# Decode attention interleaved with a feed-forward pass: scores in two runs per half batch, values in one, four buffers of turned keys

## The chip, the cores and the metric

The kernel runs on one core of one Trainium2 chip. The metric is the device time of one execution, in microseconds. The kernel before took 1261.52 us (median of 3 runs, 1261.35 to 1262.61). One more execution was recorded by the profiler; all rows below come from it.

## The reference

One layer of a hybrid decoder is computed for 512 prompt tokens and for 8 sample sequences of 4 new tokens each, with shared weights: a SwiGLU feed-forward pass, a mixer (four heads of a gated recurrence, four heads of latent attention), and a second feed-forward pass. The part that matters here is the latent attention of the sample tokens over 4096 cached positions, which lie in pages of 128:

```
past_c = cache_kv_latent[l][page_table].reshape(Bs, past_len, KV_LORA)    # 8 x 4096 x 256
past_r = cache_k_rope[l][page_table].reshape(Bs, past_len, QK_ROPE)       # 8 x 4096 x 64
...
s = (einsum('bqhr,bsr->bhqs', ql, c_kv) + einsum('bqhd,bsd->bhqs', qr, k_rope)) * scale
s = where(k_pos <= q_pos, s, -inf)
p = softmax(s, axis=-1)
return einsum('bhqs,bsr->bqhr', p, c_kv)
```

Each sequence has 16 query rows (4 tokens by 4 heads). A score row needs the 256 latent and 64 rotary elements of a cached position; the values are the same 256 latent elements. Everything is fp32.

## The kernel before, in words

Large products are made of fp32r pairs: each weight tile is loaded by SyncE into `wraw` (five buffers), cast by ScalarE into `wh` (line 248), and the rest is taken by VectorE into `wl` (line 249); three matmuls per 128 rows of the contraction then add up in a PSUM bank `acc` (lines 257, 275, 286). Four pairs of `wh` and `wl` are in rotation in the stage described here.

The decode attention is computed in a stage of its own, from about 715 to 985 us of the profiled span. There it is interleaved with the second feed-forward pass over the first 256 tokens. Two generators run side by side: `decode()` yields after each of its steps, and a loop calls the feed-forward generator `gb` so that 100 of its pieces are spread evenly over the first 94 decode steps. One piece is mostly 12 `acc` matmuls of 256 columns while gate and up columns are computed, and 15 or 18 while down columns are.

The cache is worked through in 16 half batches (class `Half`), each of 2048 positions of one sequence, held as two blocks of 128 partitions by 8 positions. For a half batch:

- `gather` starts two indirect DMAs from GpSimd per block: the rotary rows into `rraw` (four buffers, line 1360) and the latent rows into `craw` (line 1361), which rotates through seven slots that are taken over from tiles that are dead by then (`ulb`, `uhb`, `ha`, `hb`, `mb`, `q`, `dx`; the trace shows the slots' names).
- `turn(st)` transposes keys on VectorE in 32 by 32 squares into a `kh` tile (line 1370), two instructions for each of five steps. `JS` says which two of the ten groups of 32 elements a step turns; step 0 is the rotary pair, which reads `rraw`. `kh` has three buffers.
- `score(st)` multiplies one `kh` tile with the queries: 16 matmuls (32 in the trace, since each fp32 matmul is shown as two) that use the array as eight tiles of 64 rows by 32 columns (line 1382). They add up over the five steps in two banks `s`. After the last step ScalarE and VectorE copy the banks (line 1388) and VectorE takes a row maximum `mxh`.
- `peak` (lines 1394 to 1406) spreads the maxima with one matmul `pm`, reduces it, takes the exponential on ScalarE, transposes on VectorE into `pt`, and copies it in 16 small pieces into `pbuf`, 12 of them on ScalarE and 4 on VectorE.
- `value(c)` multiplies block `c` by the probabilities: 8 matmuls (16 in the trace) on four tiles of 128 rows by 32 columns (line 1415). After every second half batch `gathered` collects the sums (line 1423).

Half batches overlap. In an iteration of five steps, the half batch two iterations back is scored, one step of scores per decode step; the one three back has its `peak` in step 0 and its `value` in steps 3 and 4, and each `value` is followed by the gather of one further block. In every step one `kh` is turned for a score that comes three steps later. Within one engine instructions run in the order of a scheduler that starts from this written order and moves single instructions by its own estimate of readiness.

Of the kernel before, what the change touches and what calls it, by code (L numbers as in the profile page):

```python
# [8 lines left out]
F32 = mybir.dt.float32  # L9
# [8 lines left out]
P = 128  # L18
# [17 lines left out]
RD = 64  # L36
# [5 lines left out]
ROWS = 8  # L42
# [20 lines left out]
NW, WX = 2, 2  # L63
NDEC = 100
JS = ((8, 9), (0, 1), (2, 3), (4, 5), (6, 7))
KHB = 3
LEVELS = (32, 16, 8, 4, 2, 1)
CH = 64

# [39 lines left out]
def hybrid_step_kernel(  # L109
# [5 lines left out]
    nc = tc.nc  # L115
# [12 lines left out]
    def mk(shape, dt, tag, bufs=1, pool=None):  # L128
        return (pool or cur[-1]).tile(shape, dt, name=tag, tag=tag, bufs=bufs)
# [130 lines left out]
    def gemm(wt, act_):  # L260
        wh, wl, kt = wt
        acc = ps("acc", "acc")
        n = act_[0].shape[-1]
        mm3(acc[:, :n], [((wh[:, k], wl[:, k]), (act_[0][:, k], act_[1][:, k])) for k in range(kt)])
        return acc[:, :n]
# [139 lines left out]
    idx = mk([P, NBLK], I32, "idx")  # L405
# [147 lines left out]
    with scope("ffn0") as pool:  # L553
# [91 lines left out]
        l, r = [u[:, lo4] for u in ux], [u[:, hi4] for u in ux]  # L645
# [13 lines left out]
        for j in range(NF // 2):  # L659
# [14 lines left out]
            if j:  # L674
                H = [mk([P, 2, 2, W2], F32R, n, 3) for n in ("hh", "hl")]
# [16 lines left out]
        H = [mk([P, 2, 2, W2], F32R, n, 3) for n in ("hh", "hl")]  # L692
# [4 lines left out]
        if True:  # L697
            if True:
                sst.close()
                st = stg.enter_context(tc.tile_pool(name="st", bufs=1, side="right", reuse_waits="tile"))  # L700
# [72 lines left out]
    with scope("mix") as mx_:  # L773
# [293 lines left out]
        with scope("at2"):  # L1067
# [6 lines left out]
            with scope("kv"):  # L1074
# [46 lines left out]
                for g in range(2):  # L1121
                    w = weight([w_qr[2 * g + i] for i in range(2)], KQ)
                    a = [gemm(w, Q[x]) for x in BOTH]
# [171 lines left out]
    with scope("dec"):  # L1295
# [47 lines left out]
        NH2 = 2 * NB  # L1343

        class Half:
# [7 lines left out]
            def gather(self):  # L1353
                blk = 2 * self.n + len(self.craw)
                slot = slots[blk % len(slots)]
                craw = qt if slot == "q0" else mk([P, ROWS * R], F32, slot, pool=None if slot == "dx" else act)
                craw = craw[:, : ROWS * R].rearrange("p (a r) -> p a r", a=ROWS)
                rraw = mk([P, ROWS, RD], F32, "rraw", 4)
                off = bass.IndirectOffsetOnAxis(ap=idx[:, blk : blk + 1], axis=0)
                nc.gpsimd.indirect_dma_start(rraw.rearrange("p a r -> p (a r)"), None, pool_r, off)  # L1360
                nc.gpsimd.indirect_dma_start(craw.rearrange("p a r -> p (a r)"), None, pool_c, off)
                self.craw.append(craw)
                self.rraw.append(rraw)

            def turn(self, st):
                kh = mk([P, 2, ROWS, 2, 32], F32, "kh", KHB)
                j = JS[st][0]
                for g in range(2):
                    src = self.craw[g][:, :, j * 32 : j * 32 + 64] if j < 8 else self.rraw[g]
                    nc.vector.transpose(kh[:, g].rearrange("p a j k -> p a (j k)"), src)  # L1370
                self.kh.append(kh)
# [54 lines left out]
        def decode():  # L1426
            H = [Half(n) for n in range(NH2)]
            blocks = [h_ for h_ in H for _ in range(2)]
            ups = [(h_, st) for h_ in H for st in range(len(JS))]

            def gather(n=1):
                for h_ in blocks[:n]:
                    h_.gather()
                del blocks[:n]

            def turn():
                if ups:
                    h_, st = ups.pop(0)
                    h_.turn(st)

            for n in range(NH2 + 4):

                def at(k):
                    return H[n - k] if 0 <= n - k < NH2 else None

                for st in range(len(JS)):
                    if at(2):
                        at(2).score(st)
                    if n < 3 and st == 0:
                        gather(2 + n // 2)  # L1450
                    if st == 0 and at(3):
                        at(3).peak()
                    if st == 1 and at(4) and at(4).i:
                        at(4).gathered()
                    if st >= 3 and at(3):
                        at(3).value(at(4), st - 3)
                        gather()
                    if at(2) or n == 1 and st >= 2:
                        turn()
                    yield  # L1460

        def decode_end():
# [33 lines left out]
            nc.vector.tensor_copy(oT[1][:, NH:, HS[1] - TS :], o[:, :P].rearrange("p (h t) -> p h t", h=NH))  # L1496

        ga, gn = decode(), decode_new()
        na, ib = len(JS) * (NH2 + 2) + 4, 0
        for ia in range(na):  # L1500
# [189 lines left out]
```

## Time and profile before

| | |
|---|---|
| median of the runs | 1261.52 us |
| profiled execution, its own time | 1272.78 us |
| its span, first to last instruction | 1271.0 us |
| mean granted TensorE clock | 0.997 |
| TensorE matmul busy | 1246.2 us (98%) |
| VectorE busy | 983.3 us (77%) |
| ScalarE busy | 740.0 us (58%) |
| first and last score matmul | 719.7 and 970.6 us |

Busy time counts an engine's matmuls or operations as a union, not what they could do at their peak. TensorE's weight loads (PEld) overlap its matmuls (PE). A row of the timeline gives the start, the duration, the engine, the line and operation, output and inputs, and a count; in brackets stands the idle time before it and what ended it. "issue" means that nothing the profile shows was waited for.

### The profile page before, as it was taken

What the parts mean: (1) busy time and instruction counts of PE and PEld (TensorE: products, weight loads), DVE (VectorE), ACT (ScalarE), POOL (GpSimd) and SP (SyncE); (2) the same over time, 40 slices, a digit from 0 to 9 for tenths busy, and PEclk for the clock granted to TensorE, in tenths of its full rate; (3) what the DMA queues carried; (4) which work ended last, traced back from release to release, by engine and by line L of the source; (5) the groups of instructions that cost most, each with busy time, mean ns of one, the idle gap of its engine ahead of it and who ended that gap; (6) DMA issues with size and microseconds to landing.
All of it is one profiled execution on the core that took longest, in us unless ns stands there. A gap on an engine that the chain in (4) does not pass through costs nothing.

```text
span 1271.0 us, 30058 instructions
## 1 busy us (share of the span) xinstructions
PE 1246.2 (98%) x12390; PEld 1156.1 (91%) x12390; DVE 983.3 (77%) x1974; ACT 740.0 (58%) x1559; POOL 73.4 (6%) x80
## 2 busy tenths in 40 slices
PE   8999999999999999999999999999999999999997
PEld 7999999999999988889888887777777999999997
DVE  7897778888678888777776997888987868566665
ACT  7675545454566645547567655664655777554454
POOL 0000000000000000000001312222310000000000
PEclk9999999999999999999999999999999999999999
DMA  6233323332154222234224968768675626545451
GB/s 233 84 117 100 100 84 100 101 100 92 53 217 157 84 86 69 71 90 128 84 68 147 376 225 305 264 231 314 238 236 190 227 102 197 184 138 189 142 160 59
DMA packets 72969, 195.06 MB, mean 153 GB/s; under 512 B 12320, under 2 KB 27712, under 8 KB 68096
## 3 DMA queue, kind: packets, MB, share of 16 engines
q1 hardware_dynamic: 64368, 149.94, 36.4%
q0 software_dynamic: 7168, 41.95, 9.1%
q8 instruction: 97, 1.59, 0.5%
q10 hardware_dynamic: 1296, 1.26, 0.3%
q14 instruction: 40, 0.33, 0.1%
HBM read 183.45 MB, written 9.67 MB: 152 GB/s over the span
## 4 chain that ended last, share of the span: by engine, by line
PE 89%; ACT 5%; DVE 4%; issue 1%; DMA 0%; DVEq 0%; SPq 0%; ACTq 0%
PE acc L257 29%; PE acc L275 19%; PE dn L257 8%; PE Y L559 6%; PE X L559 4%; PE Z L559 4%; PE s L1382 4%; PE acc L715 3%; PE o L1415 3%; PE s L1195 1%; ACT wh L248 1%; PE acc L286 1%; PE pa L936 1%; DVE wl L249 1%; PE zx L824 1%
## 5 line engine op out<-in xcount | busy, mean ns | idle before, releaser
L248 ACT CAST wh<-wraw 128x1024 fp32r<-128x1024 f32 (+2 forms) x194 | 185.1, 956 | 179.2 <-PE acc L257 113.2
L249 DVE TENSOR_TENSOR wl<-wraw,wh 128x1024 fp32r<-128x1024 f32 (+2 forms) x194 | 214.7, 1108 | 88.1 <-ACT wh L248 85.6
L275 PE MATMUL acc<-uha,wh 128*128 128x256 f32 (+1 forms) x528 | 157.8, 300 | 0.9 <-ACT uha L205 0.9
L275 PE MATMUL acc<-ula,wh 128*128 128x256 f32 (+1 forms) x528 | 150.8, 286 | 0.0
L275 PE MATMUL acc<-uha,wl 128*128 128x256 f32 (+1 forms) x528 | 150.0, 285 | 0.1
L257 PE MATMUL acc<-uhb,wh 128*128 128x288 f32 (+1 forms) x432 | 128.0, 296 | 0.0
L257 PE MATMUL acc<-uhb,wl 128*128 128x288 f32 (+1 forms) x432 | 126.9, 295 | 1.0 <-DVE wl L249 0.7
L257 PE MATMUL acc<-ulb,wh 128*128 128x288 f32 (+1 forms) x432 | 127.5, 295 | 0.0
L275 PEld LDWEIGHTS acc<-uha,wh 128*128 128x128 f32 x528 | 99.4, 189 | 14.8 <-issue 13.2
L275 PEld LDWEIGHTS acc<-ula,wh 128*128 128x128 f32 x528 | 99.6, 189 | 1.4 <-issue 1.2
L275 PEld LDWEIGHTS acc<-uha,wl 128*128 128x128 f32 x528 | 99.4, 188 | 1.3 <-issue 0.7
L257 PEld LDWEIGHTS acc<-uhb,wl 128*128 128x128 f32 x432 | 81.2, 188 | 1.6 <-DVE wl L249 1.5
L257 PEld LDWEIGHTS acc<-uhb,wh 128*128 128x128 f32 x432 | 81.0, 187 | 0.2 <-ACT uhb L168 0.2
L257 PEld LDWEIGHTS acc<-ulb,wh 128*128 128x128 f32 x432 | 81.1, 188 | 0.1
L257 PE MATMUL dn<-hh,dh 128*128 128x272 f32 x256 | 74.3, 290 | 0.0
L257 PE MATMUL dn<-hh,dl 128*128 128x272 f32 x256 | 73.7, 288 | 0.0
L257 PE MATMUL dn<-hl,dh 128*128 128x272 f32 x256 | 73.6, 288 | 0.0
L1382 PE MATMUL s<-kh,q 64*32 64x128 f32 x2560 | 55.7, 275 | 0.9 <-issue 0.9
L1406 ACT COPY pbuf<-pt 32x64 f32<-32x64 f32 x192 | 46.5, 242 | 13.2 <-DVE pt L1402 10.5
L275 PE MATMUL acc<-uhb,wh 128*128 128x272 f32 x176 | 52.5, 298 | 0.0
L257 PE MATMUL acc<-hlb,wh 128*128 128x288 f32 x176 | 52.1, 298 | 0.0
L257 PE MATMUL acc<-hhb,wh 128*128 128x288 f32 x176 | 51.8, 298 | 0.0
(637 smaller groups left out, 3901.6 us busy)
## 6 DMA issues: line engine op xcount, KB each, us to landing
wraw<-w_u SPq DMA_DIRECT2D x66, 512.0 KB
wraw<-w_g SPq DMA_DIRECT2D x65, 512.0 KB
wraw<-w_d SPq DMA_DIRECT2D x40, 384.0 KB
wraw<-w_in SPq DMA_DIRECT2D x24, 512.0 KB
wraw<-w_d SPq DMA_DIRECT2D x32, 320.0 KB
wraw<-w_d SPq DMA_DIRECT2D x16, 512.0 KB
wraw<-w_o SPq DMA_DIRECT2D x16, 512.0 KB
g_S<-state SPq DMA_DIRECT2D x4, 512.0 KB
```

What stands on the lines that cost most here:

```text
L248: nc.scalar.copy(wh[:, :kt], w[:, :kt])
L249: nc.vector.tensor_tensor(wl[:, :kt], w[:, :kt], f32(wh[:, :kt]), op=ALU.subtract)
L257: nc.tensor.matmul(out, a, b, start=n == 0, stop=n == last)
L275: nc.tensor.matmul(acc[:, :n], a[:, k], b[:, k], start=k + i == 0, stop=k == kt - 1 and i == 2)
L286: nc.tensor.matmul(acc, a[:, k], b[:, k], start=k + i == 0, stop=k == kt - 1 and i == 2)
L559: nc.tensor.matmul(bank, a[p][:, k], b[q][:, k], start=first and k + n == 0, stop=k == 3 and n == 2, skip_group_check=True)
L715: nc.tensor.matmul(accs[x, d], wts[d][p][:, k], hs[k // 2][q][:, k % 2, x], start=k + n == 0, stop=k == nf - 1 and n == 2)
L824: nc.tensor.matmul(z, w[a][:, k], U[1][b][:, k], start=k + n == 0, stop=k == KD - 1 and n == 2)
L936: nc.tensor.matmul(po[es, c].rearrange("p (n m) -> p n m", m=m), kx[:, cs], up(qx[:, cs], m), start=True, stop=True, skip_group_check=True)
L1382: nc.tensor.matmul(self.s[r][c * 32 : c * 32 + 32, :P], q[rs, j], kh, start=st + jj == 0, stop=st == len(JS) - 1 and jj == 1, skip_group_c ...
L1406: (nc.scalar.copy if g else nc.vector.tensor_copy)(self.p[g * 32 : g * 32 + 32, c // 2, c % 2 * 4 : c % 2 * 4 + 4, self.i * 16 : self.i * ...
L1415: nc.tensor.matmul(o[g : g + 32, :R], self.p[:, c, a], self.craw[c][:, a], start=i + c == 0 and a < 4, stop=i + c == 2 and a >= 4, skip_gr ...
```

## The change

The scores of a half batch are no longer computed one step at a time. Steps 0, 1 and 2 are computed together in decode step 2, and steps 3 and 4 together in decode step 4, so that `kh` has to hold more tiles: four buffers instead of three. `peak` moves from decode step 0 to step 1. Both `value` calls move to decode step 4, one right after the other, each still followed by the gather of one block. The rotary rows are gathered in a function of their own, both blocks at once, after the rotary pair of the half batch before has been turned; `rraw` has two buffers instead of four. Turning starts one step earlier in iteration 1, and pauses for two steps in iteration 2.

```diff
-KHB = 3
+KHB = 4
+PEAK = 1
+RUNS = {2: (0, 1, 2), 4: (3, 4)}
...
-                rraw = mk([P, ROWS, RD], F32, "rraw", 4)
                 off = bass.IndirectOffsetOnAxis(ap=idx[:, blk : blk + 1], axis=0)
-                nc.gpsimd.indirect_dma_start(rraw.rearrange("p a r -> p (a r)"), None, pool_r, off)
                 nc.gpsimd.indirect_dma_start(craw.rearrange("p a r -> p (a r)"), None, pool_c, off)
                 self.craw.append(craw)
-                self.rraw.append(rraw)
+
+            def gather_r(self):
+                for blk in (2 * self.n, 2 * self.n + 1):
+                    rraw = mk([P, ROWS, RD], F32, "rraw", 2)
+                    off = bass.IndirectOffsetOnAxis(ap=idx[:, blk : blk + 1], axis=0)
+                    nc.gpsimd.indirect_dma_start(rraw.rearrange("p a r -> p (a r)"), None, pool_r, off)
+                    self.rraw.append(rraw)
...
                     h_.turn(st)
+                    if st == 0 and h_.n + 1 < NH2:
+                        H[h_.n + 1].gather_r()
...
                 for st in range(len(JS)):
                     if at(2):
-                        at(2).score(st)
+                        for k in RUNS.get(st, ()):
+                            at(2).score(k)
                     if n < 3 and st == 0:
+                        if n == 0:
+                            H[0].gather_r()
                         gather(2 + n // 2)
-                    if st == 0 and at(3):
+                    if st == PEAK and at(3):
                         at(3).peak()
                     if st == 1 and at(4) and at(4).i:
                         at(4).gathered()
-                    if st >= 3 and at(3):
-                        at(3).value(at(4), st - 3)
-                        gather()
-                    if at(2) or n == 1 and st >= 2:
-                        turn()
+                    if st == len(JS) - 1 and at(3):
+                        for c in range(2):
+                            at(3).value(at(4), c)
+                            gather()
+                    if n > 1 or n == 1 and st >= 1:
+                        if n != 2 or st >= 2:
+                            turn()
                     yield
```

On TensorE, the stretch from the fifth peak matmul to the values of that half batch stood like this before (each `...` is a stretch of `acc` matmuls of the feed-forward pass, of 12 or 24):

```order
L1394 MATMUL pm<-ident,mxh 128x128
...
L1382 MATMUL s<-kh,q_8177 32x128 x16
L1423 MATMUL o<-q_8177,q_8811 128x32 x2
...
L1382 MATMUL s<-kh,q_8177 32x128 x16
...
L1382 MATMUL s<-kh,q_8177 32x128 x16
L1415 MATMUL o<-uhb,pbuf 32x256 x8
...
L1382 MATMUL s<-kh,q_8177 32x128 x16
L1415 MATMUL o<-ha,pbuf 32x256 x8
```

and stands like this now:

```order
L1400 MATMUL pm<-ident,mxh 128x128
L1429 MATMUL o<-q_8177,q_8811 128x32 x2
...
L1388 MATMUL s<-kh,q_8177 32x128 x48
...
L1388 MATMUL s<-kh,q_8177 32x128 x32
L1421 MATMUL o<-uhb,pbuf 32x256 x8
L1421 MATMUL o<-ha,pbuf 32x256 x8
```

The number of matmuls is the same; 16 score matmuls that stood apart are now runs of 48 and 32, and the two value runs touch. Over the whole program the 1280 score matmuls stand in 80 runs before and in 37 now; the first half batch is still cut into five, since the scheduler places its runs between other work.

On VectorE, the stretch of the seventh peak, from the reduction of `pm` to the copies into `pbuf`, stood like this before:

```order
L1396 TENSOR_REDUCE q_8177<-pm 128x16
L1370 STREAM_TRANSPOSE kh<-ulb 128x512
L1399 SCALAR_TENSOR_TENSOR mq,mbd<-q_8177 128x16
L1370 STREAM_TRANSPOSE kh<-uhb 128x512
L1370 STREAM_TRANSPOSE kh<-ulb 128x512
L1402 STREAM_TRANSPOSE pt<-q_8177 128x256
L1424 COPY q_8811<-o 128x4x16
L1406 COPY pbuf<-pt 32x4x16 x4
L1370 STREAM_TRANSPOSE kh<-uhb 128x512
```

and now:

```order
L1402 TENSOR_REDUCE q_8177<-pm 128x16
L1430 COPY q_8811<-o 128x4x16
L1405 SCALAR_TENSOR_TENSOR mq,mbd<-q_8177 128x16
L350 TENSOR_TENSOR sil<-acc,rna 128x256
L1408 STREAM_TRANSPOSE pt<-q_8177 128x256
L1412 COPY pbuf<-pt 32x4x16 x4
L1376 STREAM_TRANSPOSE kh<-ulb 128x512
L1376 STREAM_TRANSPOSE kh<-uhb 128x512
L1376 STREAM_TRANSPOSE kh<-rraw 128x512 x2
```

Three transposes of keys stood between the reduction and `pbuf`; now they stand before it or behind it.

## The prediction

> **What bounds the kernel now.** First the page: busy time and the chain of work that ended last.
>
> ```profile
> span 1271.0 us, 30058 instructions
> PE 1246.2 (98%) x12390; PEld 1156.1 (91%) x12390; DVE 983.3 (77%) x1974; ACT 740.0 (58%) x1559; POOL 73.4 (6%) x80
> PE 89%; ACT 5%; DVE 4%; issue 1%; DMA 0%; DVEq 0%; SPq 0%; ACTq 0%
> ```
>
> TensorE is busy for 98% of the span and holds 89% of the chain. Busy does not mean that it works at its peak, so the question is what its time in the decode stage is made of. I cut that stage by what the feed-forward pass does beside it: gate and up columns in the first, third and fifth row, down columns in the others (columns: stretch, length, PE, PEld, DVE and ACT busy with counts, POOL, clock, DMA share, GB/s).
>
> ```profile
> 715.00:758.00 43.00, 41.93 (x661) 35.28 (x667) 41.76 (x88) 25.74 (x57) 11.20 (x11) 1.00 0.80 282
> 758.00:789.00 31.00, 29.48 (x488) 23.92 (x496) 23.36 (x46) 17.31 (x47) 7.62 (x8) 1.00 0.80 278
> 789.00:853.00 64.00, 63.66 (x1163) 50.08 (x1152) 56.64 (x131) 39.40 (x108) 17.47 (x16) 1.00 0.77 276
> 853.00:885.00 32.00, 31.28 (x499) 24.33 (x483) 25.41 (x52) 15.40 (x38) 8.86 (x8) 1.00 0.73 262
> 885.00:942.00 57.00, 56.69 (x982) 44.55 (x988) 49.61 (x112) 33.15 (x93) 14.44 (x13) 1.00 0.68 237
> 942.00:963.00 21.00, 21.00 (x407) 16.73 (x391) 19.80 (x43) 11.02 (x25) 0.00 (x0) 1.00 0.75 252
> ```
>
> TensorE is busy throughout, VectorE is second: 97% of the first row (41.76 of 43), 89% of the third, 75% of the second. So TensorE's time is the bound nearly everywhere, with VectorE close behind beside gate and up columns. The granted clock is 1.00, so no time is hidden there.
>
> Third, the timeline on PE, for what a score run costs. Three runs, of 14, 50 and 32 matmuls as the trace counts them, with the `acc` matmuls around them:
>
> ```profile
> 728.82 0.28 PE L275 MATMUL acc<-uha,wl 128*128 128x256 f32 x1
> 729.03 1.06 PE L1382 MATMUL s<-kh,q 64*32 64x128 f32 x50
> 730.02 0.39 PE L275 MATMUL acc<-uha,wl 128*128 128x256 f32 x1
> 730.24 0.27 PE L275 MATMUL acc<-uha,wh 128*128 128x256 f32 x1
> ...
> 732.61 0.28 PE L275 MATMUL acc<-uha,wl 128*128 128x256 f32 x1
> 732.82 0.44 PE L1382 MATMUL s<-kh,q 64*32 64x128 f32 x14
> 733.19 0.39 PE L275 MATMUL acc<-uha,wh 128*128 128x256 f32 x1
> 733.42 0.29 PE L275 MATMUL acc<-ula,wh 128*128 128x256 f32 x1
> ...
> 790.86 0.28 PE L275 MATMUL acc<-ula,wh 128*128 128x256 f32 x1
> 790.98 0.28 PE L275 MATMUL acc<-uha,wl 128*128 128x256 f32 x1
> 791.19 0.67 PE L1382 MATMUL s<-kh,q 64*32 64x128 f32 x32
> 791.78 0.38 PE L275 MATMUL acc<-uha,wh 128*128 128x256 f32 x1
> 792.01 0.28 PE L275 MATMUL acc<-ula,wh 128*128 128x256 f32 x1
> ```
>
> `acc` matmuls follow each other every 0.12 us (790.86, 790.98). From the last one before a run to the second one behind it, two such steps (0.24) would pass without a run. The run of 32 takes 792.01 - 790.98 = 1.03 us, so it costs 0.79; the run of 14 costs 0.81 - 0.24 = 0.57. Eighteen more matmuls cost 0.22 us, 12 ns each. Thirty-two at that rate are 0.39 us; the other 0.40 us is paid once per run, at the change from `acc` to score matmuls and back (0.21 us into the run instead of 0.12, and 0.23 us between the first two `acc` matmuls behind it).
>
> **The change, part by part.** *Scores in two runs.* The order of the program has 80 score runs before and 37 now: 43 fixed parts fall away. If a longer run goes on at 12 ns, each is worth 0.40 us, 17.2 us in all. The run of 50 is the nearest row for a longer one: from its start to the next `acc` it takes 0.99 us, against 0.59 for the run of 32, so its 18 extra matmuls cost 0.40 instead of 0.22. It is the one run that stands apart and crosses from one `kh` tile to the next, which every joined run does. A joint then costs 0.18 back and saves 0.22: 9.5 us in all. I take 0.26 per joint, nearer to the only row that has one: 11.2 us.
>
> *Values in one run.* A score run with one value run behind it, and from the groups between 718 and 975 us the mean duration of a value matmul (386 ns):
>
> ```profile
> 796.82 0.28 PE L275 MATMUL acc<-uha,wl 128*128 128x256 f32 x1
> 797.03 0.67 PE L1382 MATMUL s<-kh,q 64*32 64x128 f32 x32
> 797.62 1.07 PE L1415 MATMUL o<-dx,pbuf 128*32 128x256 f32 x16
> 798.63 0.39 PE L275 MATMUL acc<-uha,wh 128*128 128x256 f32 x1
> 798.85 0.28 PE L275 MATMUL acc<-ula,wh 128*128 128x256 f32 x1
> ...
> L1415 PE MATMUL o<-uhb,pbuf 128*32 128x256 f32 x80 | 8.0, 386 | 0.6
> ```
>
> 2.03 - 0.24 - 0.79 = 1.00 us for the 16 value matmuls. They start (1.07 - 0.39) / 15 = 45 ns apart, 0.73 us for 16; 0.27 us is the joint. Of two value runs per half batch one loses its joint, in 15 half batches: 4.0 us. If the second block's first matmul brings the joint back, nothing.
>
> *The peak one step later* leaves its score run and stands between `acc` matmuls. The last half batch's peak already does:
>
> ```profile
> 973.25 0.28 PE L275 MATMUL acc<-uha,wl 128*128 128x256 f32 x1
> 973.37 0.38 PE L1394 MATMUL pm<-ident,mxh 128*128 128x128 f32 x2
> 973.51 0.37 PE L275 MATMUL acc<-uha,wh 128*128 128x256 f32 x1
> 973.71 0.28 PE L275 MATMUL acc<-ula,wh 128*128 128x256 f32 x1
> ```
>
> 0.46 - 0.24 = 0.22 us, no dearer. The chain behind it must end in `pbuf` before the values:
>
> ```profile
> 804.42 0.49 PE L1394 MATMUL pm<-ident,mxh 128*128 128x128 f32 x2
> 808.63 3.07 ACT L1406 COPY pbuf<-pt 32x64 f32<-32x64 f32 x12 [0.69 <-DVE pt L1402]
> 811.75 1.07 PE L1415 MATMUL o<-uhb,pbuf 128*32 128x256 f32 x16
> ```
>
> It took 7.28 us to the last copy (811.70) and is all used up: the first values start 7.33 us behind the peak. Now 36 `acc` matmuls (4.3 us), a run of 96 (about 2) and one of 64 (about 1) stand between them, again some 7.3 us; the second block follows 1 us behind the first instead of a step. In return three key transposes leave the chain on VectorE, about 2 us. I set this to nothing; if each half batch waits 0.5 us there, 8 us are lost.
>
> *Fourth `kh` buffer, gathers.* Both keep their counts: 160 transposes, 96 gathers. A turned key now has at least two decode steps before its score instead of three; behind the transpose that waits for a freed buffer on VectorE stand the next `wl` and so the next weights. Latent gathers still land five steps ahead of their first transpose. GpSimd, on which a rotary gather stood in front of the latent ones, is idle for most of the stage. Nothing, as long as VectorE keeps up.
>
> *Does VectorE keep up?* Its work stays while the stage shrinks. TensorE's 15.2 us over some 250 us are 6%. Beside down columns VectorE has 7.6 and 6.6 us to spare for 1.9 each: full gain. In the first row it has 1.2 us left for about 2 wanted, in the last 1.2 for 1.3. In the two long rows it would give 3.9 of 7.4 and 3.4 of 7.4; its queue is in order and waits for ScalarE's casts there, so I let a quarter, 1.8 us, be lost. Together 2.7 us.
>
> **Sum:** 11.2 + 4.0 - 2.7 = 12.5 us. The profiled execution would go from 1272.78 (span 1271.0) to about 1260.3. It lies 11.3 us above the median of 1261.52; I carry the difference over unscaled (1% of it is 0.1 us): **1249 us**.
>
> **Rivals.**
> (1) *Full gain.* Joints cost nothing (17.2 + 4.0) and VectorE follows: 1240 to 1244. For it: in steady state keys are turned well ahead, which they were not at 729 us. Against: VectorE at 89%.
> (2) *Mostly eaten.* VectorE becomes the bound beside gate and up columns, or values wait for `pbuf`. If only the down columns (3.8) and a quarter of the other 11.4 us gain, 6.7 us remain: 1255. The run of 50 gives a second way there: if every matmul beyond 32 costs 22 ns, a run of 96 takes 0.79 + 1.41 where three runs took 2.37, a run of 64 takes 1.49 where two took 1.58, and with the values' 0.27 a half batch gains 0.53 us: 8.5 us in all, 1253. For it: VectorE's 97% in the first row. Against: the idle time of the third and fifth.
> (3) *Long runs starve.* TensorE's loads already pause inside some value runs:
>
> ```profile
> 860.10 0.29 PEld L1415 LDWEIGHTS o<-uhb,pbuf 128*32 128x32 f32 x5 [0.20 <-issue]
> 861.00 0.18 PEld L1415 LDWEIGHTS o<-uhb,pbuf 128*32 128x32 f32 x5 [0.61 <-issue]
> 861.77 0.16 PEld L1415 LDWEIGHTS o<-uhb,pbuf 128*32 128x32 f32 x4 [0.59 <-issue]
> 862.51 0.14 PEld L1415 LDWEIGHTS o<-uhb,pbuf 128*32 128x32 f32 x2 [0.58 <-issue]
> ```
>
> [...] The dense part of a half batch is now two bursts of 96 matmuls each, twice the longest before. One extra pause per burst, 30 x 0.6 = 18 us, eats the gain of 15.2: that is the point from which it decides. With two, 36 - 15 = 21 us slower: 1282. Against it: the run of 50 has no pause.
> [...]
> (4) *Nothing.* Stalls move and the sum cancels: within 0.2%.
>
> **How the numbers follow.** Forecast 0.50 (1244 to 1254), rival 1 0.14, rival 2 0.17, rival 4 0.08, rival 3 0.11. 0.2% is 2.5 us, about what can be told from no change. Faster by more takes the forecast, rival 1 and all but 0.01 of rival 2: 0.80. Same 0.09, slower 0.11. The unknown costs span 17.2 + 4.0 (1240) to 9.5 + 0 - 2.7 (1255), and half of the possible wait for `pbuf` (4 us) more: 1240 to 1259, which leaves out rivals 3 and 4 and a little of rival 1.
>
> **What would show it.** PE timeline: runs of 96 and 64 followed by 32 values; from the last `acc` before to the second behind, 2.1 to 2.3 us for the run of 96 (1.8 if rival 1 holds, over 3 with pauses) and 3.2 to 3.6 for the other. Stage windows: VectorE over 93% beside gate and up columns. Waits: `wl` for `wh` shorter; if `o` for `pbuf` or `s` for `kh` shows more than a few us, rival 2. More than 40 pauses of 0.6 us on PEld would make the prediction wrong, and so would a last score run that comes no earlier than now.

## The result, and the profile after

The changed kernel takes 1256.88 us (median of 6 runs, 1255.17 to 1258.28), the kernel before, run beside it, 1261.60 us (6 runs, 1260.99 to 1262.61). The ratio is 0.9961 with a 95% interval of 0.9950 to 0.9972: 4.7 us faster, clear of the noise, but well under half of the 12.5 us that the sum gave.

First the page of the changed kernel: span, busy times and the chain of work that ended last.

```profile
span 1255.5 us, 30042 instructions
PE 1227.1 (98%) x12390; PEld 1158.5 (92%) x12390; DVE 982.1 (78%) x1974; ACT 740.6 (59%) x1559; POOL 73.6 (6%) x80
PE 79%; DVE 10%; ACT 8%; issue 3%; DMA 1%; DVEq 0%; SPq 0%; ACTq 0%
```

The chain has moved: TensorE held 89% of it before and holds 79% now, VectorE went from 4 to 10%, ScalarE from 5 to 8%. TensorE is also less busy, by 8.6 us against the repeat of the kernel before that is shown below (1235.7), more than the 4.7 us that came off the time. The profiled execution took 1257.24 us, right among the timed runs. That of the kernel before (1272.78) had not been, which matters below.

Next the PE timeline: a score run of 96, and a run of 64 with both value runs behind it.

```profile
755.75 0.28 PE L277 MATMUL acc<-uha,wl 128*128 128x256 f32 x1
755.96 1.59 PE L1388 MATMUL s<-kh,q 64*32 64x128 f32 x96
757.49 0.39 PE L288 MATMUL acc<-hha,wh 128*128 128x256 f32 x1
757.71 0.28 PE L288 MATMUL acc<-hla,wh 128*128 128x256 f32 x1
...
951.93 0.28 PE L277 MATMUL acc<-uha,wl 128*128 128x256 f32 x1
952.14 1.16 PE L1388 MATMUL s<-kh,q 64*32 64x128 f32 x64
953.22 1.07 PE L1421 MATMUL o<-ulb,pbuf 128*32 128x256 f32 x16
954.11 1.05 PE L1421 MATMUL o<-uhb,pbuf 128*32 128x256 f32 x16
955.09 0.38 PE L277 MATMUL acc<-uha,wh 128*128 128x256 f32 x1
955.31 0.28 PE L277 MATMUL acc<-ula,wh 128*128 128x256 f32 x1
```

From the last `acc` before to the second one behind, less 0.24 for two `acc` steps: the run of 96 costs 757.71 - 755.75 - 0.24 = 1.72 us, the other 955.31 - 951.93 - 0.24 = 3.14. A peak that doesn't wait costs 0.22. Three runs of 32 cost 2.37 before, and two runs of 32 with 16 values each 3.58. So the work on TensorE did get cheaper, as the prediction had it.

Where the rest went is seen in what TensorE waits for in the stage (waits of PE from 715 to 960 us: in total, times, longest).

```profile
PE pm L1400 <- DVE mxh L1396: 1.6, 3, 1.1
PE o L1421 <- issue: 1.5, 2, 0.9
PE acc L277 <- issue: 1.1, 1, 1.1
PE acc L288 <- ACT hha L170: 1.0, 1, 1.0
PE acc L288 <- DVE hla L171: 0.7, 1, 0.7
```

The first row is a wait for VectorE. The two rows of "issue" are pauses before which nothing in the profile was waited for: one in each of two value runs, and one between two `acc` matmuls (921.51 us). The last two rows stand where up columns end and down columns begin, whose matmuls need the hidden values as a pair: `hha`, made by ScalarE, and `hla`, made by VectorE. At both places the copies into `pbuf` are queued ahead of the pair. At 849.59 us `hha` had its input `sil` since 846.11, but stood on ScalarE behind twelve such copies (846.07 to 849.10); at 762.11 us `hla` stood on VectorE behind a `wl` and four of them (759.95 to 761.60). In the stage as a whole ScalarE's `hha` waits much longer for VectorE than in the repeat of the kernel before (3.1 us there):

```profile
ACT hha L170 <- DVE sil L353: 13.2, 10, 2.7
```

The rows of PE count only its idle time; what a late operand costs in all is taken from the timeline, in the account after the experiments.

### The profile page after: what moved, and what is told of

It is laid out like the page before. It is cut to its first block, busy times and chain, and to the rows that moved or that the text cites. A ratio compares the mean times of both kernels' runs of the same rounds, so it can differ in the third digit from the quotient of the medians.

```text
span 1255.5 us, 30042 instructions
## 1 busy us (share of the span) xinstructions
PE 1227.1 (98%) x12390; PEld 1158.5 (92%) x12390; DVE 982.1 (78%) x1974; ACT 740.6 (59%) x1559; POOL 73.6 (6%) x80
## 4 chain that ended last, share of the span: by engine, by line
PE 79%; DVE 10%; ACT 8%; issue 3%; DMA 1%; DVEq 0%; SPq 0%; ACTq 0%
PE acc L259 29%; PE acc L277 14%; PE dn L259 8%; PE Y L561 6%; PE X L561 4%; PE Z L561 4%; PE acc L717 3%; DVE wl L251 3%; DVE kh L1376 2%; ACT pbuf L1412 2%; ACT wh L250 2%; PE s L1388 1%; PE s L1197 1%; PE pa L938 1%; PE o L1421 1%
## 5 line engine op out<-in xcount | busy, mean ns | idle before, releaser
L259 PE MATMUL acc<-hhb,wl 128*128 128x288 f32 x176 | 51.4, 294 | 0.0
L277 PE MATMUL acc<-uhb,wl 128*128 128x272 f32 x176 | 51.1, 290 | 0.0
```

What stands on the lines that cost most here:

```text
L259: nc.tensor.matmul(out, a, b, start=n == 0, stop=n == last)
L277: nc.tensor.matmul(acc[:, :n], a[:, k], b[:, k], start=k + i == 0, stop=k == kt - 1 and i == 2)
```

## The experiments

Twelve kernels ran. In all of them the stage goes from the first score matmul to the last peak matmul, and the account of each is given in one table at the end of this section.

**The kernel before, once more.** Nothing is edited.

> The kernel before, unchanged, profiled a second time. Theory A: the profiled execution that the prediction was worked out from was 11 us longer than the timed ones because it held pauses of 0.6 us in the supply of TensorE's instructions (about 11 us of them between 715 and 945 us) that other executions do not have; then this profile lasts 1260 to 1264 us and shows fewer than a third of those pauses. Rival B: profiling this kernel always adds them; then it lasts 1270 to 1275 us and shows them again. The timed runs stay at 1261 to 1262 us under both.

Measured: 1261.49 us (1259.94 to 1262.49, 10 runs), ratio 0.9999 (0.9989 to 1.0008). The profile of this execution:

```profile
span 1258.2 us, 30058 instructions
PE 1235.7 (98%) x12390; PEld 1151.8 (92%) x12390; DVE 982.3 (78%) x1974; ACT 740.6 (59%) x1559; POOL 74.6 (6%) x80
PE 87%; DVE 7%; ACT 5%; issue 1%; DMA 0%; DVEq 0%; SPq 0%; ACTq 0%
```

Its span is 12.8 us shorter than that of the profile shown first. The waits of PEld that were released by nothing the profile shows, in the value runs from 718 to 975 us of the first profile:

```profile
PEld o L1415 <- issue: 12.9, 38, 0.6
```

and from 715 to 960 us of this one:

```profile
PEld o L1415 <- issue: 4.6, 23, 0.2
PE pm L1394 <- DVE mxh L1390: 0.5, 2, 0.3
```

The pauses of 0.6 us are gone; the longest is 0.2. These waits of the loads are 8.3 us shorter; counted by the timelines, the groups with value matmuls are 12.5 us cheaper, nearly all of the 12.8. What the loads paused for is not shown; that it was the supply of TensorE's instructions, as the theory has it, no view says. In this timeline a score run of 32 costs 0.79 us and one with 16 values 1.79, with hardly an exception. The stage takes 242.0 us. The first profile had caught an execution with stalls that the timed runs, 11 us shorter, can hardly have had, and the windows show what that did to VectorE's share (stretch, length, PE, PEld, DVE, ACT and POOL busy, clock, DMA share, GB/s):

```profile
715.00:758.00 43.00, 42.07 (x692) 36.17 (x692) 42.53 (x90) 27.72 (x66) 11.33 (x11) 1.00 0.82 291
758.00:789.00 31.00, 31.00 (x522) 25.66 (x521) 25.52 (x53) 17.89 (x47) 7.88 (x8) 1.00 0.85 300
789.00:848.00 59.00, 58.50 (x1087) 46.71 (x1087) 53.51 (x122) 38.67 (x108) 17.95 (x16) 1.00 0.78 276
848.00:876.00 28.00, 28.00 (x471) 23.00 (x470) 24.96 (x49) 13.49 (x30) 8.58 (x8) 1.00 0.82 290
876.00:926.00 50.00, 50.00 (x934) 39.88 (x933) 45.86 (x107) 32.12 (x91) 15.04 (x13) 1.00 0.73 257
```

The five stretches are roughly the same parts of the program as the first five rows of the prediction, and shorter. VectorE's idle time sums to 0.47 + 5.48 + 5.49 + 3.04 + 4.14 = 18.6 us, where the first profile had 30.2 (1.24 + 7.64 + 7.36 + 6.59 + 7.39). The bounds are up to 5 us off. Cut at the same `acc` matmuls as the prediction's rows (714.0, 755.9, 784.3, 846.3, 875.1 and 930.5 us) the idle time is 20.0 us, with 0.4 in the first stretch; so a third of what the first profile showed came with its pauses.

**The values in one run, alone.** On the kernel before:

```diff
-                    if st >= 3 and at(3):
-                        at(3).value(at(4), st - 3)
-                        gather()
+                    if st == len(JS) - 1 and at(3):
+                        for c in range(2):
+                            at(3).value(at(4), c)
+                            gather()
```

> The kernel before, with one edit: both value runs of a half batch stand together behind the last score step. Theory (a joint between score and value matmuls costs TensorE 0.27 us, 15 of them fall away, and VectorE is not yet short): 4.0 us faster, 1257.5. Rival (the first matmul of the second block brings the joint back, or the blocks' later gather and pbuf wait eat it): 1261 to 1262, and the pair of value runs takes more than 1.75 us in the timeline.

Measured: 1260.93 us, ratio 0.9998 (0.9989 to 1.0007): nothing. Its PE timeline:

```profile
884.07 0.28 PE L275 MATMUL acc<-uha,wl 128*128 128x256 f32 x1
884.28 0.67 PE L1382 MATMUL s<-kh,q 64*32 64x128 f32 x32
884.88 1.07 PE L1415 MATMUL o<-mb,pbuf 128*32 128x256 f32 x16
885.77 1.05 PE L1415 MATMUL o<-q,pbuf 128*32 128x256 f32 x16
886.74 0.39 PE L275 MATMUL acc<-uha,wh 128*128 128x256 f32 x1
886.97 0.27 PE L275 MATMUL acc<-ula,wh 128*128 128x256 f32 x1
```

The group costs 886.97 - 884.07 - 0.24 = 2.66 us. Apart, the same work costs 1.79 + 1.00. A joint between value runs is therefore worth 0.13 us, half of what was taken: the second run starts 0.89 us behind the first, where its 16 matmuls need 0.73. Fifteen times 0.13 is 2.0 us; the stage got 1.1 us shorter, longer waits at the peaks and one late `hla` took the rest.

**Scores in two runs, with the peak where it was.** The changed kernel with `PEAK = 0` and the values back in steps 3 and 4:

```diff
-PEAK = 1
+PEAK = 0
...
-                    if st == len(JS) - 1 and at(3):
-                        for c in range(2):
-                            at(3).value(at(4), c)
-                            gather()
+                    if st >= 3 and at(3):
+                        at(3).value(at(4), st - 3)
+                        gather()
```

> The changed kernel without two of its parts: the peak stays in decode step 0, the value runs in steps 3 and 4. What is left are scores in two runs, four buffers of turned keys and the rotary gathers ahead. By TensorE's sum alone (43 joints of 0.26 us): 11.2 us faster, 1250.3. Theory (VectorE holds the stage back whatever TensorE saves): far less, 1256 to 1259, with 92 to 96% of VectorE's time busy beside gate and up columns. Rival (what holds the change back is the value runs' place behind the peak's chain): 1251 to 1253, better than the whole change.

Measured: 1268.97 us, ratio 1.0059 (1.0046 to 1.0073), slower than the kernel before. None of the three expectations had that. Its score runs cost 1.72 us like those of the changed kernel; TensorE loses the time at the peaks, where its waits for `mxh` sum to 11.4 us.

**The whole change, with the peak where it was.** Only the first two lines of that diff.

> The changed kernel with the peak in decode step 0 as before, so that its chain to pbuf has a step more (about 1.7 us) and the peak shares a run's joint again where scores stand next to it. If the chain behind the peak holds the values back (8% of the stage's chain of waits goes through pbuf): 2 to 4 us faster than the changed kernel, 1253 to 1255. If not: 1256 to 1258.

Measured: 1268.23 us, ratio 1.0057 (1.0043 to 1.0071), 11 us above the changed kernel; again no expectation had that. Waits of PE, 715 to 970 us, and the worst peak with what VectorE did ahead of it:

```profile
PE pm L1400 <- DVE mxh L1396: 13.1, 9, 2.9
```

```profile
802.10 0.25 DVE L1394 COPY q<-s 128x128 f32<-128x128 f32 x1
802.28 0.69 DVE L1376 STREAM_TRANSPOSE kh<-hb 128x512 f32<-128x512 f32 x1
802.89 0.38 DVE L1396 TENSOR_REDUCE mxh<-q 128x1 f32<-128x256 f32 x1
...
803.42 0.76 PE L1400 MATMUL pm<-ident,mxh 128*128 128x128 f32 x2 [2.75 <-DVE mxh L1396]
```

The peak needs the row maximum of the scores, whose last run stands in step 4, one step ahead, as before the change. But VectorE comes to copy the score bank 2.8 us behind the last score on the mean, against 1.3 in the repeat of the kernel before, with key transposes ahead of the copy and of the maximum in its queue. TensorE stands for 2.75 us at this place, with everything behind the peak. The later peak, which the prediction had put down as "no dearer", is what makes the longer score runs pay at all.

**Scores in two runs and the later peak, values apart.** Only the second part of that diff.

> The changed kernel with its value runs back in steps 3 and 4: scores in two runs, and the peak in step 1. With the peak in step 0 the same kernel took 1269 us, and its peak matmuls waited up to 3.2 us for VectorE's maximum (mxh). Theory (the peak's place is what decides; joined values save only 0.13 us per half batch, as their 2.66 us against 0.79 + 1.00 + 1.00 in the timeline of the kernel with the values alone): 1257 to 1260, peaks waiting for mxh by 3 us in all instead of 11. Rival (the first values, a step earlier, now wait for pbuf, whose chain takes some 7 us): 1262 to 1270, with o waiting for pbuf by 0.5 us or more per half batch.

Measured: 1257.16 us, ratio 0.9964 (0.9951 to 0.9976), the same as the whole change. PE's waits for `mxh` are 0.8 us in all, and those for `pbuf` 0.7:

```profile
PE pm L1400 <- DVE mxh L1396: 0.8, 3, 0.4
PE o L1421 <- ACT pbuf L1412: 0.7, 2, 0.3
```

So the gain is that of the score runs with the later peak. Joining the values adds nothing to it.

**The later peak alone.** On the kernel before:

```diff
-                    if st == 0 and at(3):
+                    if st == 1 and at(3):
```

> The kernel before with the peak in step 1, nothing else. The first values stand in step 3, so that the chain from the peak to pbuf (7.3 us) has a step less, about 2.2 us. Theory (the chain fills all the time it has): 0.5 to 2 us more per half batch, 1268 to 1290. Rival (the chain has room once the pauses of the first profile are gone): 1260 to 1263.

Measured: 1266.58 us, ratio 1.0036 (1.0024 to 1.0049), between the two expectations. The values in step 3 come too early for the shorter way to `pbuf`:

```profile
823.76 1.24 PE L1415 MATMUL o<-hb,pbuf 128*32 128x256 f32 x16 [1.07 <-ACT pbuf L1406]
```

That happens in three half batches, whose groups take 1.0, 1.3 and 1.3 us longer. The peak's move is a loss by itself and a need beside the long score runs.

**Half of the key transposes left out.** The keys of the second block are not turned, and its scores use the first block's keys, so that the attention these two kernels compute is another one. VectorE has 80 transposes less; TensorE has the same number of matmuls. On the kernel before and on the changed one:

```diff
-                for g in range(2):
+                for g in range(1):
...
-                            kh = self.kh[st][rs, c // 2, c % 2 * 4 : c % 2 * 4 + 4, jj]
+                            kh = self.kh[st][rs, 0, c % 2 * 4 : c % 2 * 4 + 4, jj]
```

> The kernel before, with the keys of the second block of each half batch not turned (the scores of that block use the first block's turned keys): 80 transposes of 0.62 us less on VectorE, 50 us of work, TensorE's instructions the same in number and order of kind. Theory A (TensorE bounds the kernel before, VectorE the changed one): 1257 to 1261 us, little gained. Rival B (VectorE bounds both): below 1252 us.

> The changed kernel with the keys of the second block of each half batch not turned, as in the run with half the turns of the kernel before. Theory A (TensorE saves 17 us but VectorE, now the bound, holds most of it back): 1240 to 1246 us, 11 us or more below the changed kernel's 1257, and 13 us or more below the kernel before with half the turns. Rival C (the missing gain is lost elsewhere: in waits for pbuf, in pauses of the instruction supply, in the stage behind): not below 1253 us.

Measured: on the kernel before 1260.73 us, ratio 0.9989 (0.9980 to 0.9999); on the changed one 1248.13 us, ratio 0.9889 (0.9868 to 0.9911). VectorE loses about 43 us of work in both. Before the change that is worth 0.8 us, so VectorE hardly held TensorE up there; after it, 8.8 us (four runs, 1245.02 to 1250.62), so then it did. Theory A had the direction; its numbers for the changed kernel (1246 or less, 11 and 13 us) were each missed by a little.

Not all of the 8.8 us is VectorE's. The scheduler, with fewer transposes to place, also changed the order on TensorE: the scores of the first two half batches stand in five runs instead of nine, and with the peaks and values among them they cost 10.0 us instead of 13.0, by the count of the account below. And two pauses of unknown cause, 2.5 us together, stay in this profile too. Between the two kernels with half of the turns the change is worth 12.6 us. That this is nearly the 12.5 of the sum is chance: those 12.5 have VectorE's 2.7 taken off already, and in this pair pauses and the other order, which the sum does not have, count with it.

How late VectorE runs can be read directly: from the end of a half batch's last score matmul to VectorE's copy of that bank. In the repeated profile of the kernel before:

```profile
899.02 0.67 PE L1382 MATMUL s<-kh,q 64*32 64x128 f32 x32
...
901.62 0.28 DVE L1388 COPY q<-s 128x128 f32<-128x128 f32 x1
```

and in the changed kernel, at the worst place:

```profile
907.63 1.16 PE L1388 MATMUL s<-kh,q 64*32 64x128 f32 x64
...
913.49 0.25 DVE L1394 COPY q<-s 128x128 f32<-128x128 f32 x1
...
914.80 0.46 PE L1400 MATMUL pm<-ident,mxh 128*128 128x128 f32 x2 [1.10 <-DVE mxh L1396]
```

1.93 us there, 4.70 here. Over the half batches the mean is 1.3 us before, 3.0 in the changed kernel, and 1.5 in the changed kernel with half of the turns.

**Less work for VectorE, at ScalarE's cost.** In the changed kernel all copies to `pbuf` and both copies of the score banks on ScalarE:

```diff
-                    (nc.vector.tensor_copy if r else nc.scalar.copy)(self.e[:, r * P : r * P + P], self.s[r][:, :P])
+                    nc.scalar.copy(self.e[:, r * P : r * P + P], self.s[r][:, :P])
...
-                        (nc.scalar.copy if g else nc.vector.tensor_copy)(self.p[...], src)
+                        nc.scalar.copy(self.p[...], src)
```

> The changed kernel with the 4 copies into pbuf that VectorE makes per half batch, and the second copy of e, on ScalarE: VectorE loses 5 operations or about 1.05 us per half batch, 17 us in all, ScalarE gains about 1.25 us per half batch. Theory (VectorE's work is what holds the change back by about 9 us): 1249 to 1252, less if the chain of copies behind the peak gets longer on ScalarE. Rival (not the amount of VectorE's work, but the order of its queue): 1256 to 1258, no change. Rival (ScalarE, 15 us of waits for sil in the stage, is as close to the bound): 1257 to 1262, values waiting for pbuf.

Measured: 1260.80 us, ratio 0.9996 (0.9987 to 1.0005): the gain is gone. VectorE's busy time fell by 13 us, ScalarE's rose by 15, and now the feed-forward pass waits for ScalarE's part of its hidden values:

```profile
763.44 0.39 PE L288 MATMUL acc<-hha,wh 128*128 128x256 f32 x1 [2.67 <-ACT hha L170]
```

The gate between up columns and down columns runs through VectorE and ScalarE by turns (`sil`, `sit`, `hha`, `hla`), so work pushed from one to the other delays the same chain.

**The same copies on GpSimd.** The four copies to `pbuf` that VectorE makes go to GpSimd, the bank copy to ScalarE:

```diff
-                    (nc.vector.tensor_copy if r else nc.scalar.copy)(self.e[:, r * P : r * P + P], self.s[r][:, :P])
+                    nc.scalar.copy(self.e[:, r * P : r * P + P], self.s[r][:, :P])
...
-                        (nc.scalar.copy if g else nc.vector.tensor_copy)(self.p[...], src)
+                        (nc.scalar.copy if g else nc.gpsimd.tensor_copy)(self.p[...], src)
```

> The changed kernel with VectorE relieved of small copies and nothing left out: the four copies per half batch into pbuf that VectorE made go to GpSimd, and its copy of the second score bank to ScalarE. That takes 4 x 0.2 + 0.25 = 1.05 us per half batch from VectorE, 17 us in all. Theory A: 1248 to 1253 us. Rival C: 1256 to 1258 us, or slower if GpSimd's copies delay the values.

Measured: 1264.57 us, ratio 1.0039 (1.0021 to 1.0057). The values wait for the copies:

```profile
PE o L1421 <- POOL pbuf L1412: 8.3, 6, 2.7
```

Such a copy takes GpSimd 0.33 us where VectorE needs 0.18, and it stands in one queue with the gathers: the same view has GpSimd's copies waiting for gathers of latent rows to land, up to 7.4 us at a time.

**A quarter of the `wl` splits on GpSimd.**

```diff
-        nc.vector.tensor_tensor(wl[:, :kt], w[:, :kt], f32(wh[:, :kt]), op=ALU.subtract)
+        (nc.gpsimd if home is None and not staged and wx and wcnt[0] % 4 == 0 else nc.vector).tensor_tensor(wl[:, :kt], w[:, :kt], f32(wh[:, :kt]), op=ALU.subtract)
```

> The changed kernel with the subtraction wl of every fourth weight of the stage on GpSimd: some 15 operations of 1.085 us leave VectorE, 16 us in the stage, and ScalarE gets nothing. Theory (VectorE's work is what keeps the change from its whole gain): 1249 to 1254. Rival (GpSimd takes so much longer for one that TensorE waits for wl): 1258 or more, with acc waiting for POOL wl.

Measured: 1266.65 us, ratio 1.0046 (1.0032 to 1.0061). The edit moved 38 splits in the whole kernel, 15 of them in the stage. The group of those left on VectorE, from 715 to 960 us, and from the timeline one of them beside one on GpSimd:

```profile
L251 DVE TENSOR_TENSOR wl<-wraw,wh 128x1024 fp32r<-128x1024 f32 (+2 forms) x44 | 57.0, 1299 | 4.0 <-ACT wh L250 3.9
...
812.23 2.38 POOL L251 TENSOR_TENSOR wl<-wraw,wh 128x1024 fp32r<-128x1024 f32 x1
812.47 3.22 DVE L251 TENSOR_TENSOR wl<-wraw,wh 128x1024 fp32r<-128x1024 f32 x1
```

The splits left on VectorE became dearer on the mean, 1299 ns instead of 1085 in the changed kernel (both over three sizes): 44 x 0.21 = 9 us of the 16 that left came back. The mean hides how. In the timeline six of the 44 lie over most of a split on GpSimd and take 2.56 to 3.22 us; the 36 that overlap none take 1.06 us on the mean, no more than before. What holds the six up no run shows. TensorE's waits are those for VectorE and ScalarE again (`mxh` 2.9 us, `hha` 2.1), not for GpSimd's `wl`, as the rival had it. At equal work the stage is no longer than in the kernel before; the rest of the loss lies behind it (4.1 us against the repeat), where the edit moved splits too, and its cause is not shown.

**Scores a step earlier.** To give the maximum a step more, both score runs and the turning move one step ahead:

```diff
-RUNS = {2: (0, 1, 2), 4: (3, 4)}
+RUNS = {1: (0, 1, 2), 3: (3, 4)}
...
-                        if n != 2 or st >= 2:
+                        if n != 2 or st >= 1:
```

> The changed kernel with the scores' two runs and the turning of keys one decode step earlier (runs in steps 1 and 3 instead of 2 and 4). The maximum mxh then has a step more before the peak. Theory (the peaks' waits for mxh, 2.7 us in the changed kernel's timeline, are given back, and VectorE's amount of work still holds the rest): 1253 to 1256. Rival (score runs now wait for kh, which has a step less): 1257 to 1265. If VectorE takes all of it elsewhere: 1256 to 1258.

Measured: 1260.41 us, ratio 0.9995 (0.9986 to 1.0003), in the rival's range but not for its reason: no score run waits for `kh`. The peaks no longer wait, but the values do, behind a chain to `pbuf` that has become longer on VectorE:

```profile
PE o L1421 <- ACT pbuf L1412: 2.6, 2, 1.3
```

The exponential on ScalarE (`q`, line 1406) waits 47.2 us for VectorE's `mq` in the stage, where it waited 12.9 in the changed kernel. And the value runs, which stand apart from the score runs here, cost 0.20 us more with them: 1.28 + 2.06 us for a half batch's 64 scores and 32 values instead of 3.14.

**The account.** Taken from each PE timeline. "Runs" is the sum, over all groups of matmuls other than `acc`, of the time from the last `acc` before to the second `acc` behind less 0.24; waits inside a group count with it. "`acc`" is the rest of the stage. The number of `acc` matmuls in it is not the same everywhere: where the peak stands in step 1, the last peak comes one piece later, and the stage holds 1186 of them instead of 1174. Those 12 are 1.4 us of work, to be taken off `acc` and off the stage where the two kinds are compared; their rows are marked with a star. "Late" is how much of `acc` is delay: the sum, over steps from one `acc` matmul to the next of more than 0.16 us, of what they take beyond 0.119 us, the second steps behind other groups left out.

| kernel | median, us | stage | runs | `acc` | late |
|---|---|---|---|---|---|
| before (repeated) | 1261.49 | 242.0 | 103.3 | 138.7 | 0 |
| values in one run alone | 1260.93 | 240.9 | 102.3 | 138.6 | 0.1 |
| later peak alone * | 1266.58 | 246.5 | 106.5 | 140.0 | 0 |
| scores in two runs alone | 1268.97 | 248.2 | 107.9 | 140.4 | 1.5 |
| scores in two runs, later peak * | 1257.16 | 238.0 | 97.6 | 140.4 | 0.1 |
| the change * | 1256.88 | 237.6 | 93.0 | 144.5 | 4.2 |
| the change, peak in step 0 | 1268.23 | 248.9 | 106.2 | 142.7 | 3.9 |
| the change, scores a step earlier * | 1260.41 | 240.7 | 98.3 | 142.4 | 1.9 |
| the change, copies on ScalarE * | 1260.80 | 241.0 | 93.0 | 148.0 | 7.7 |
| the change, copies on GpSimd * | 1264.57 | 243.6 | 101.4 | 142.2 | 1.9 |
| the change, some `wl` on GpSimd * | 1266.65 | 243.2 | 96.6 | 146.6 | 6.2 |
| before, half of the turns | 1260.73 | 241.1 | 102.5 | 138.6 | 0 |
| the change, half of the turns * | 1248.13 | 228.1 | 87.9 | 140.2 | 0 |

At equal work the stage differences follow the medians to about 2 us, but for the kernel with copies on GpSimd (2.9) and the one with `wl` on GpSimd (5.4); the edit of the last reaches beyond the stage. At equal work the change makes the stage 5.8 us shorter: 242.0 + 1.4 - 237.6.

Two rows carry the reading. From "scores in two runs, later peak" to the whole change the runs get 4.6 us cheaper and the `acc` stretches 4.1 us longer. Nearly all of that lies at four places. 2.5 us are the two late pairs of hidden values (0.95 at 762, 1.5 at 850 us), and 1.6 us are two pauses before which nothing was waited for (1.3 at 921.51, 0.3 at 893.75). With half of the turns no `acc` matmul is late, and the waits at the peaks are gone; the runs get 5.1 us cheaper, of which 2.9 are these waits and most of the rest is the other order of the first two half batches.

## Why the prediction was right or wrong

The direction was right and the time inside the range. The size was not: 1249 forecast, 1256.9 measured, 4.7 us gained instead of 12.5. The step that failed is what comes off TensorE's saving: it was put at 2.7 us, for VectorE alone, and is 9.6 in the stage, about half of it at VectorE's and ScalarE's late operands and half in pauses that the sum had at nothing. By the prediction's own steps:

- **Joints between score runs: right, mis-sized a little.** Taken at 0.26 us with bounds of 0.22 and 0.40. The run of 96 gives (3 x 0.79 - 1.72) / 2 = 0.33, the run of 64 about 0.31. At 0.32, 43 joints are 13.8 us instead of 11.2. The run of 50, on which the lower bound rested, was no model of a long run: beyond 32 matmuls each costs (1.72 - 0.79) / 64 = 14.5 ns, not 22.
- **Joint between values: half as large**, 0.13 instead of 0.27, 2.0 us instead of 4.0.
- Both together are 15.8 us where the sum had 15.2. The timelines agree: with the waits inside groups taken out (0.9 us before, 6.1 after) the runs went from 102.3 to 86.9, 15.4 us less.
- **The peak: 0.22 us, as said**, but the step missed that its old place would have become dear: in step 0 the peaks wait 13 us for `mxh`, in step 1 some 3 us, by the timeline's groups. It also missed that the peak's copies into `pbuf` would now be queued ahead of `hha` and `hla` at two ends of up columns.
- **`pbuf`, the fourth `kh` buffer, the gathers: nothing, as said.** TensorE's waits in the changed kernel have no row for `pbuf` or `kh`.
- **VectorE takes 2.7 us back: the term that failed.** It is 4.5 us: 2.0 more at the peaks, which wait for VectorE's `mxh`, and 2.5 at the late `hha` and `hla`. That VectorE's load is behind these is shown by the half turns, with which both vanish, and by its lag of 3.0 us instead of 1.3. Part of the miss is the idle time that was read from the first profile (30.2 us in five stretches, 20.0 in the repeat): the prediction knew that its execution lay 11.3 us above the median and wrote "I carry the difference over unscaled". That held for TensorE's prices, whose rows were clean, and failed for VectorE's room. But it is not the whole: with 0.4 us of room in the first row and 0.6 in the last (930.5 to 950.3 us of the repeat) the same working would give an estimated 4.1 us, by the same guess of a quarter for the long rows, and it would look for the loss in the wrong place. VectorE is idle for 15 us in the same five stretches of the changed kernel (715.9 to 928.8 us), and TensorE waits for it all the same, at the few places where one operand of a chain comes late.
- **Pauses: nothing in the sum, 4.3 us measured.** 2.7 us of them are in value runs, 1.6 between `acc` matmuls (921.51 and 893.75 us).
- **Long runs starve (rival 3): true for two bursts of thirty, its reason not shown.** In the fifth and sixth half batch the loads of the first value run stop behind a score run of 64, in the fifth with `pbuf` complete since 806.82 (twelve copies on ScalarE, from 803.74 on, 3.08 us). From the PEld timeline of the changed kernel:

```profile
807.73 0.15 PEld L1421 LDWEIGHTS o<-uhb,pbuf 128*32 128x32 f32 x6 [0.20 <-issue]
809.04 0.35 PEld L1421 LDWEIGHTS o<-uhb,pbuf 128*32 128x32 f32 x9 [1.16 <-issue]
```

  Each makes its group 1.3 us longer, 2.7 us in all. The kernel with half of the turns has two as well, in the fifth half batch and, within a score run, in the seventh. What the loads waited for there no run shows. In the one execution recorded of each kernel, neither the kernel before in its repeat nor "scores in two runs, later peak", whose values stand apart, has a pause of "issue" of over 0.43 us on PEld in the stage. The pauses may thus be part of why joining the values gains nothing, but this has not been repeated.
- **Rival 2 came closest**: its first way (VectorE the bound beside gate and up columns, 6.7 us left, 1255) names half of the mechanism and misses the time by 2 us. That it comes so near is partly luck, since the other half of the loss is the pauses.

The sum with the measured terms: 15.4 less 2.0 (peaks), 2.5 (`hha` and `hla`), 2.7 (pauses in value runs), 1.9 (pauses and small delays between `acc` matmuls) and 0.5 of small waits in other groups is 5.8 us, the stage's difference at equal work. The medians differ by 4.7. The 1.1 us between the two are not explained; outside the stage, where nothing was changed, single executions also differ by some us (the first score comes 718.5 us after the start in the repeat, 719.7 in the first profile of the same kernel and 720.5 in the changed one).

Of what the prediction said would show it: the run of 96 takes 1.96 us with its two `acc` steps (said 2.1 to 2.3, or 1.8 for rival 1), the other 3.38 (said 3.2 to 3.6). For VectorE beside gate and up columns in the changed kernel the windows have

```profile
715.00:758.00 43.00, 42.44 (x695) 37.60 (x695) 41.46 (x82) 25.05 (x55) 9.52 (x10) 1.00 0.71 246
789.00:848.00 59.00, 57.16 (x1159) 49.48 (x1158) 54.07 (x122) 38.53 (x108) 17.59 (x16) 1.00 0.78 278
876.00:926.00 50.00, 47.27 (x920) 41.29 (x911) 45.85 (x105) 32.41 (x91) 14.81 (x14) 1.00 0.76 269
```

96, 92 and 92%, where over 93 was said. The kernel before already had 99, 91 and 92% in the repeated profile, where half of VectorE's turns were worth only 0.8 us, so this sign could not have told the two apart: the busy share does not say whether an operand comes in time. VectorE's wait for ScalarE's `wh` did become shorter, as said (16.3 us in the repeat, 3.9 now).

What stays open: what the loads pause for, and whether the pauses of the changed kernel are in its other executions too; each kernel was recorded once, the kernel before twice. Open is also whether the amount of VectorE's work or the order of its queue decides, since each trial that took work off it without leaving any out made another chain longer. No version that ran beats the changed kernel; the one with its values apart equals it.

## What to carry to other kernels

Before a sum is made from a profile, compare the profiled execution's own time with the timed runs. Here it was 1% longer; prices read from clean rows held, but the idle time of the second-busiest engine was half as much again as in a repeat. When the busiest engine is relieved, the busy share of the second one does not tell what it will hold back: it was 91 to 92% beside the long stretches both where it cost nothing and where it cost several us. Look for the operands that one chain delivers just in time, and take work off the second engine in a trial, even by leaving part of it out; then compare the order of the instructions too, since the scheduler may have changed more than was meant. When stretches of two kernels are compared, count the instructions in them first. A change made of several moves can consist of parts that each lose by themselves (the later peak +5 us, the longer score runs +7) and only pay together.

## What the hardware showed that was not expected

- Two executions of the same program differ by 12.8 us of span, and 8.3 us of it are waits of the value matmuls' loads that nothing in the profile explains: 38 of up to 0.6 us in the one, 23 of up to 0.2 us in the other.
- A score run of 32 costs 0.79 us in both profiles of the kernel before, one of 96 costs 1.72 in the changed kernel: 0.40 us once, and 12 to 14.5 ns per matmul.
- Two value runs with the same tiling and nothing between them still pay 0.16 us at their seam, in the kernel with the values in one run alone and in the changed one (0.89 us from start to start against 0.73).
- A subtraction of 128 x 1024 took 2.46 us on GpSimd in the kernel with some `wl` there, and 1.21 on VectorE in the changed kernel. Six of VectorE's splits that lay over most of one of GpSimd's took 2.56 to 3.22 us; the 36 that overlapped none took 1.06 us on the mean (three sizes), where the changed kernel has 1.085.
